# The experts' weights in pieces of 2048 columns, three in flight, with the small operations queued behind stated splits

## The chip, the cores and the metric

The kernel runs on one core of a Trainium2 chip. The metric is the device time in microseconds of one execution of the whole program; lower is better.

## What is computed

A two-layer encoder trunk on 256 tokens of width 1024: in each layer a token mixer with three attention branches, a cross-attention into 256 memory tokens, and a SwiGLU feed-forward part, each followed by a residual and a layer norm. The feed-forward part of the first layer is dense; in the second, every token goes to two of eight experts of hidden width 2816. Only that last part is touched by the change:

```python
def swiglu(t, w_gu, w_down):
    a, g = jnp.split(t @ w_gu, 2, axis=-1)
    return (jax.nn.silu(a) * g) @ w_down
...
    out = jnp.zeros_like(t)
    for e in range(N_EXPERTS):
        out = out + gate[:, e:e + 1] * swiglu(t, w_gu[e], w_down[e])
```

All of it is float32. The kernel reaches that precision with three matmuls in the chip's reduced 32-bit format for each product: every operand is split into a high half (`hi`, a rounded copy) and a low half (`lo`, what the copy lost), and hi x hi, hi x lo and lo x hi are summed.

## The kernel before

The weights lie in memory packed in units, one contiguous load each. `unit` (L184) loads one unit into a `raw` tile (L193), cuts it into pieces, and makes for each piece a hi tile by a ScalarE copy (L203) and a lo tile by a VectorE subtraction (L207). The hi tiles rotate through six places of 1024 columns per partition, the lo tiles through six more, both in the pool `wp`; a place is written again when TensorE has read what was in it. The piece is 1024 columns whatever the unit's shape: two rows of blocks of 512 columns, or four rows of 256. Until the end of the first expert's first step each subtraction is cut in two (`self.cuts`), afterwards it is one instruction.

`experts` (L789) walks over eight experts in six steps j. In a step `up` (L845) makes the gate part `pg` and the linear part `pa` of 512 hidden columns (256 in the sixth step) from the gathered tokens `xg`: each is a chunk of two units of four rows of blocks, so a step has four units. A unit of 512 columns is 2048 columns per partition and gives 12 matmuls of 512 columns; in the sixth step it is 1024 and gives 12 matmuls of 256. `down` (L878) takes the hidden columns of the step before, already turned round in `hT`, through two units (output halves `py`): 2048 columns and 12 matmuls each, in the sixth step two rows of blocks, 1024 columns and 6 matmuls. The order is therefore: up of step 0, up of step 1, down of step 0, up of step 2, down of step 1, and so on across the experts; the sixth `down` of one expert follows the first `up` of the next. Before the first, third, fifth and seventh expert `gather` (L811) fetches the tokens of two experts by matmuls and evacuates them on ScalarE (L835) and VectorE (L836).

What turns `pg` and `pa` into `hT` is put off: `up` appends the function `rest` to the list `self.later`, and `flush` (L872) runs the whole list. `rest` is silu on ScalarE (L862), the product on VectorE (L863), four transposes on TensorE (L866) and a split on ScalarE and VectorE (L243, L244). `flush` is called in `up` once, after the first chunk's splits, and in `down` after the splits of each unit. So the work of step j runs between the splits and the matmuls of the first `down` unit that follows it. After an expert's last `down`, `scatter` (L904) is put off in the same way; it splits the two output halves, scaled by the gate (L246, L247), and after every second expert puts off `add`, 16 matmuls (L921) and four additions (L924) that bring the results back to token order.

Each engine runs its instructions in the order in which they are queued. That order comes from the order of the program text and from a scheduler that may let an instruction whose inputs are late be passed by later ones. All loads are issued on the SP queue.

The three matmuls of a product are:

```python
        t.matmul(out, a[0], b[0], start=first, stop=False, **kw)
        t.matmul(out, a[0], b[1], start=False, stop=False, **kw)
        t.matmul(out, a[1], b[0], start=False, stop=last, **kw)
```

With weights as the moving operand (`a` the tokens, `b` the weights), the first needs the hi tile alone, the second the lo tile, the third the hi tile again.

Of the kernel before, what the change touches and what calls it, by code (L numbers as in the profile page):

```python
# [153 lines left out]
class K:  # L154
    def __init__(self, ctx, tc, I, out):
        self.tc, self.nc, self.I, self.out = tc, tc.nc, I, out
        nc = self.nc
        P = lambda **kw: ctx.enter_context(tc.tile_pool(**kw))
        self.const = P(name="const", bufs=1)
        self.wp = P(name="wp", bufs=3)  # L160
        self.tp = P(name="tp", bufs=1)
        self.nT = 0
        self.xp = P(name="xp", bufs=2)
        self.sm = P(name="sm", bufs=4)
        self.mm = P(name="mm", bufs=3, space=PSUM)
        self.ps = P(name="ps", bufs=2, space=PSUM)
        c = self.const
        self.idn = c.tile([128, 128], FT, name="idn")
        nc.sync.dma_start(self.idn, I["eye"])
        self.half = c.tile([128, 1], FT, name="half")  # L170
        nc.vector.memset(self.half, -0.5)

        self.raws = [(self.wp, "raw")]

        self.cuts = 2
        self.base = {}
        o = 0
        for l in range(DEPTH):
            for p in MIX:
                self.base[p.name, l] = o  # L180
                o += p.size


    def unit(self, src, base, pk, c, g, blocks=False):  # L184


        nc = self.nc
        cn, (k0, kn) = pk.chunks[c][1], pk.groups[g]
        n = kn * cn
        pool, tag = self.raws[0]  # L190
        self.raws.append(self.raws.pop(0))
        raw = pool.tile([128, kn, cn], FT, name="raw", tag=tag, bufs=3 if pool is self.wp else 1)
        nc.sync.dma_start(raw.rearrange("p k c -> p (k c)"),  # L193
                          bass.AP(tensor=src.tensor, offset=src.offset + base + pk.off[c, g], ap=[[n, 128], [1, n]]))
        kp = kn if blocks else 1024 // cn
        out = []
        for a, b in [(0, c) for c in range(cn // 128)] if blocks else [(k, 0) for k in range(0, kn, kp)]:
            ks = slice(a, min(kn, a + kp))
            cs = slice(b * 128, b * 128 + 128) if blocks else slice(0, cn)
            shape = [128, ks.stop - a, cs.stop - cs.start]  # L200
            hi = self.wp.tile(shape, FR, name="hi", tag="hi", bufs=6)
            lo = self.wp.tile(shape, FR, name="lo", tag="lo", bufs=6)
            nc.scalar.activation(hi, raw[:, ks, cs], AF.Copy)  # L203
            m = -(-shape[1] // self.cuts)
            for k in range(0, shape[1], m):
                kk = slice(k, min(k + m, shape[1]))
                nc.vector.tensor_tensor(lo[:, kk], raw[:, a:][:, kk, cs], f32(hi[:, kk]), op=OP.subtract)  # L207
            out.append((k0 + a, shape[1], hi, lo))
        return out

# [7 lines left out]
    def mm3(self, out, a, b, first, last, **kw):  # L218

        t = self.nc.tensor  # L220
        t.matmul(out, a[0], b[0], start=first, stop=False, **kw)  # L221
        t.matmul(out, a[0], b[1], start=False, stop=False, **kw)  # L222
        t.matmul(out, a[1], b[0], start=False, stop=last, **kw)  # L223

    def tm(self, ps, xT, units, t0, KT=8, first=True):

# [562 lines left out]
    def experts(self, c, pos, gs, xs, acc, A, early=()):  # L789

        down, self.later = None, []
        ahead = self.gather(c, 0, pos, xs, A)
        for e in range(E):
            if e % 2 == 0:
                pair = ahead
            one = dict(pair, e=e, i=e % 2, xe=[pair["xg"][e % 2][:, z] for z in range(2)])
            for j in range(6):
                if e == 1 and j == 0:
                    self.raws = [z for z in self.raws if z not in early]
                hT = self.up(one, j, A)  # L800
                self.cuts = 1
                if down:
                    self.down(*down, gs, acc, A)
                down = (one, j, hT)
                if e % 2 and e < E - 1 and j == 1:
                    ahead = self.gather(c, e + 1, pos, xs, A)
        self.down(*down, gs, acc, A)
        while self.later:
            self.flush()

    def gather(self, c, e, pos, xs, A):  # L811

# [32 lines left out]
    def up(self, x, j, A):  # L845

        nc, I = self.nc, self.I
        base = x["e"] * (P_GU.size + P_DN.size)
        n = P_GU.chunks[2 * j][1]
        nb = n // 128  # L850
        pg = self.mm.tile([128, 512], FT, name="pm", tag="mm")
        u = self.chunk(I["we"], base, P_GU, 2 * j + 1)
        self.flush()
        self.tm(pg[:, :n], x["xe"], u, 0)
        u = self.chunk(I["we"], base, P_GU, 2 * j)
        pa = self.mm.tile([128, 512], FT, name="pm", tag="mm")
        self.tm(pa[:, :n], x["xe"], u, 0)
        hT = [A.tile([128, 4, CAP], FR, name="hT" + s) for s in "hl"]

        def rest():  # L860
            h = A.tile([128, 512], FT, name="h", bufs=1)
            nc.scalar.activation(h[:, :n], pa[:, :n], AF.Silu)  # L862
            nc.vector.tensor_tensor(h[:, :n], h[:, :n], pg[:, :n], op=OP.mult)  # L863
            p = self.ps.tile([128, 4, 128], FT, name="pht", tag="t")
            for b in range(nb):
                nc.tensor.transpose(p[:, b], h[:, b * 128:b * 128 + 128], self.idn)  # L866
            self.split(p[:, :nb], *(z[:, :nb] for z in hT))

        self.later.append(rest)
        return hT  # L870

    def flush(self):  # L872

        later, self.later = self.later, []
        for f in later:
            f()

    def down(self, x, j, hT, gs, acc, A):  # L878

        nc, I = self.nc, self.I  # L880
        e, i = x["e"], x["i"]
        base = e * (P_GU.size + P_DN.size) + P_GU.size
        if j == 0:
            self.py = [self.ps.tile([128, 512], FT, name="py", tag="s") for _ in range(2)]
        for cc in range(2):
            u = self.unit(I["we"], base, P_DN, cc, j)
            self.flush()
            for k0, kn, hi, lo in u:
                for k in range(kn):
                    kk = k0 + k  # L890
                    self.mm3(self.py[cc], [z[:, kk - 4 * j] for z in hT], (hi[:, k], lo[:, k]), kk == 0, kk == 21)
        if j == 0:

            p = self.ps.tile([128, 2], FT, name="pgt", tag="t")
            for t in range(2):
                nc.tensor.matmul(p, x["sl"][:, t, i], gs[:, t, e], start=not t, stop=bool(t))
            g2 = self.sm.tile([128, 2], FT, name="g2")
            nc.vector.tensor_copy(g2, p)
            self.g = self.sm.tile([128, 1], FT, name="g1")
            nc.vector.tensor_tensor(self.g, g2[:, 0:1], g2[:, 1:2], op=OP.add)  # L900
        if j == 5:
            self.later.append(lambda: self.scatter(x["st"], e, acc, A))

    def scatter(self, st, e, acc, A):  # L904

# [20 lines left out]
                        self.stats(acc, t, cc)  # L926

        if i:
            self.later.append(add)

    def finish(self, acc, A, name):
        o = self.tp.tile([128, 2, D], FT, name="o" + name, tag=self.xgs[0])
# [6 lines left out]

    def moe(self, x, xT):  # L940
        nc, tc = self.nc, self.tc
        with tc.tile_pool(name="moec", bufs=1) as C:
            acc = x
            with tc.tile_pool(name="moe0", bufs=2) as A:
                pos, gs, xs = self.route(x, xT, C, A)
                nc.scalar.activation(acc, x, AF.Copy, scale=ALPHA)
                T = [f"T{(self.nT + i) % 2}{s}" for i in range(2) for s in "hl"]
                self.xgs = T[:3]

                early = [(self.tp, T[2])] + [(A, "ys" + s) for s in "hl"]  # L950
                self.raws = [(self.wp, "raw")] * 3 + [(A, f"raw{i}") for i in range(5)] + [(self.tp, T[3])] + early
                self.experts(0, pos, gs, xs, acc, A, early)
                self.raws = [(self.wp, "raw")]
                self.finish(acc, A, "a")
            over = nc.values_load(self.over[0:1, 0:1], min_val=0, max_val=S)
            with tc.If(over > CAP):
                with tc.tile_pool(name="moe1", bufs=2) as A:
                    self.experts(1, pos, gs, xs, acc, A)
                    self.finish(acc, A, "b")

    def run(self):
# [7 lines left out]
                self.stats(x, t, i)  # L969
        xT = self.ln_all(x, 0, gb)  # L970
        with ExitStack() as ctx:
            for l in range(DEPTH):
                self.mixer(l, x, xT)
                with tc.tile_pool(name=f"cr{l}", bufs=1) as A:
# [34 lines left out]
```

## Time and profile before

| what | value |
|---|---|
| median of three runs | 1654.68 us (1654.38 to 1655.45) |
| profiled execution, its own time | 1654.94 us |
| its span in the trace | 1652.8 us |
| TensorE matmul, weight load, busy | 97%, 85% |
| VectorE, ScalarE, GpSimd, busy | 80%, 62%, 2% |
| granted TensorE clock, mean | 0.992 |
| read from memory | 418.61 MB, 254 GB/s over the span |

The trace calls TensorE's matmuls PE and its weight loads PEld, VectorE DVE, ScalarE ACT, GpSimd POOL; L207 is line 207 of the kernel. Matmuls are pipelined and their ends are modelled, so their starts say more than their durations. The experts' stage fills the second half of the span, from about 852 us on. Idle time of an engine is put down to the instruction that released it.

### The profile page before, as it was taken

The numbers are of one execution on the slowest core, as the hardware profiler recorded it, in microseconds if no ns is written. First come the engines' busy times: TensorE is split into PE (matmuls) and PEld (weight loads), VectorE is DVE, ScalarE is ACT, GpSimd is POOL, SyncE is SP. The second block draws the span as 40 slices with busy tenths as digits, with TensorE's granted clock in tenths as the row PEclk, the third lists the DMA queues.
The fourth block names the chain that finished last, engine by engine and source line by source line (L and its number), as shares of the span: only waits on it lengthen the run. The fifth ranks groups of instructions, "written<-read, shape, count | busy, mean of one in ns | idle before, by whom it ended". The sixth has DMA issues, their size and how long they took to land.

```text
span 1652.8 us, 24729 instructions
## 1 busy us (share of the span) xinstructions
PE 1607.9 (97%) x9507; PEld 1408.8 (85%) x9507; DVE 1317.8 (80%) x1918; ACT 1022.2 (62%) x1362; POOL 33.4 (2%) x28
## 2 busy tenths in 40 slices
PE   6999999999999999999979999999999999999996
PEld 6999999899998889999868888888888878888785
DVE  7877685765555986777689999998989888989896
ACT  5665444454443575545458777777777677767773
POOL 1100000000000200000000000000000000000000
PEclk9999999999999999999979999999999999999998
DMA  7434564465545533455578888989889898898982
GB/s 272 141 105 152 189 232 167 143 229 180 188 171 198 186 123 131 161 203 205 192 320 328 316 352 321 393 308 382 330 322 372 327 400 325 336 373 314 400 328 84
DMA packets 65647, 421.36 MB, mean 255 GB/s; under 512 B 7664, under 2 KB 8560, under 8 KB 19568
## 3 DMA queue, kind: packets, MB, share of 16 engines
q1 hardware_dynamic: 65520, 419.69, 68.1%
q8 instruction: 77, 1.26, 0.3%
q14 instruction: 50, 0.41, 0.1%
HBM read 418.61 MB, written 1.05 MB: 254 GB/s over the span
## 4 chain that ended last, share of the span: by engine, by line
PE 92%; DVE 5%; issue 1%; ACT 1%; DMA 1%; POOL 0%; SPq 0%; DVEq 0%; ACTq 0%
PE pm L222 20%; PE pm L221 20%; PE pm L223 20%; PE py L223 5%; PE py L222 5%; PE py L221 5%; PE psc L341 2%; DVE lo L207 2%; PE ptr L370 1%; PE pht L866 1%; PE pd L221 1%; PE pd L223 1%; PE pd L222 1%; PE pg L830 1%; PE pp L221 1%; PE pp L222 1%
## 5 line engine op out<-in xcount | busy, mean ns | idle before, releaser
L207 DVE TENSOR_TENSOR lo<-raw,hi 128x1024 fp32r<-128x1024 f32 (+2 forms) x1020 | 935.3, 956 | 187.9 <-ACT hi L203 173.1
L203 ACT ACTIVATE hi<-raw 128x1024 fp32r<-128x1024 f32 x770 | 785.5, 1057 | 311.1 <-PE pm L222 92.1
L222 PE MATMUL pm<-lo,xg 128*128 128x512 f32 (+1 forms) x768 | 286.5, 373 | 2.2 <-DVE lo L207 1.8
L221 PE MATMUL pm<-hi,xg 128*128 128x512 f32 (+1 forms) x768 | 286.4, 373 | 0.0
L223 PE MATMUL pm<-hi,xg 128*128 128x512 f32 (+1 forms) x768 | 285.7, 372 | 0.0
L223 PE MATMUL pm<-xTh,lo 128*128 128x256 f32 x928 | 264.5, 285 | 0.0
L221 PE MATMUL pm<-xTh,hi 128*128 128x256 f32 x928 | 264.4, 285 | 0.0
L222 PE MATMUL pm<-xTl,hi 128*128 128x256 f32 x928 | 264.3, 285 | 0.0
L222 PEld LDWEIGHTS pm<-xTl,hi 128*128 128x128 f32 x928 | 177.8, 192 | 1.1
L221 PEld LDWEIGHTS pm<-xTh,hi 128*128 128x128 f32 x928 | 177.7, 191 | 1.0
L223 PEld LDWEIGHTS pm<-xTh,lo 128*128 128x128 f32 x928 | 177.9, 192 | 0.7
L222 PEld LDWEIGHTS pm<-lo,xg 128*128 128x128 f32 x768 | 144.7, 188 | 30.4 <-DVE lo L207 5.5
L221 PEld LDWEIGHTS pm<-hi,xg 128*128 128x128 f32 x768 | 144.7, 188 | 26.6 <-ACT hi L203 1.3
L223 PEld LDWEIGHTS pm<-hi,xg 128*128 128x128 f32 x768 | 144.7, 188 | 24.8
L221 PE MATMUL py<-hi,hTh 128*128 128x512 f32 x352 | 140.7, 400 | 0.0
L223 PE MATMUL py<-hi,hTl 128*128 128x512 f32 x352 | 140.6, 399 | 0.0
L222 PE MATMUL py<-lo,hTh 128*128 128x512 f32 x352 | 139.6, 397 | 0.0
L862 ACT ACTIVATE h<-pm 128x512 f32<-128x512 f32 (+1 forms) x48 | 27.0, 562 | 121.7 <-PE pm L223 121.7
L222 PEld LDWEIGHTS py<-lo,hTh 128*128 128x128 f32 x352 | 66.1, 188 | 14.7 <-DVE lo L207 0.4
L223 PEld LDWEIGHTS py<-hi,hTl 128*128 128x128 f32 x352 | 66.0, 188 | 14.6
L221 PEld LDWEIGHTS py<-hi,hTh 128*128 128x128 f32 x352 | 66.2, 188 | 13.6
L863 DVE TENSOR_TENSOR h<-h,pm 128x512 f32<-128x512 f32 (+1 forms) x48 | 30.7, 640 | 44.8 <-ACT h L862 44.8
(292 smaller groups left out, 2273.2 us busy)
## 6 DMA issues: line engine op xcount, KB each, us to landing
raw<-in_we SPq DMA_DIRECT2D x240, 1024.0 KB, 6.9
raw<-in_wm SPq DMA_DIRECT2D x84, 1024.0 KB, 4.8
raw<-in_wf SPq DMA_DIRECT2D x32, 1024.0 KB, 4.9
raw<-in_we SPq DMA_DIRECT2D x48, 512.0 KB, 4.9
gb<-in_lnv SPq DMA_DIRECT2D x14, 512.0 KB, 4.7
raw<-in_wm SPq DMA_DIRECT2D x4, 832.0 KB, 5.3
memr<-in_memT SPq DMA_DIRECT2D x3, 1024.0 KB, 4.8
bias<-in_bias SPq DMA_DIRECT2D x8, 256.0 KB, 4.2
```

The costliest lines, as they stand in the source:

```text
L203: nc.scalar.activation(hi, raw[:, ks, cs], AF.Copy)
L207: nc.vector.tensor_tensor(lo[:, kk], raw[:, a:][:, kk, cs], f32(hi[:, kk]), op=OP.subtract)
L221: t.matmul(out, a[0], b[0], start=first, stop=False, **kw)
L222: t.matmul(out, a[0], b[1], start=False, stop=False, **kw)
L223: t.matmul(out, a[1], b[0], start=False, stop=last, **kw)
L341: self.nc.tensor.matmul(p[:, t], q[i][a][:, t * 128:(t + 1) * 128], k[i][b], start=i + a + b == 0, stop=i == n - 1 and a == 1)
L370: nc.tensor.transpose(pt[:, kt, t * 128:(t + 1) * 128], e[:, t, kt * 128:(kt + 1) * 128], self.idn)
L830: nc.tensor.matmul(p[i][:, k % 2], xs[i][:, t, k * 128:k * 128 + 128], sl[:, t].rearrange("p a b -> p (a b)"), start=not t, stop=bool(t))
L862: nc.scalar.activation(h[:, :n], pa[:, :n], AF.Silu)
L863: nc.vector.tensor_tensor(h[:, :n], h[:, :n], pg[:, :n], op=OP.mult)
L866: nc.tensor.transpose(p[:, b], h[:, b * 128:b * 128 + 128], self.idn)
```

## The change

`unit` takes the piece's size from `self.piece`: 1024 columns with six places as before in all other layers, 2048 columns with three places in the experts' stage, where `moe` opens a new pool `hl1` for the hi and lo tiles. Each unit of the experts is then one piece, one ScalarE copy and one VectorE subtraction (two in the first step of the first expert), whether it has 2048 columns or 1024. In the other layers the hi and lo tiles lie in a pool `hl` of their own instead of in `wp`.

`up` calls `flush` after the splits of each of its four units. What is put off now has a count, the number of flushes until it runs: silu and product run in the third (that of the next `up`'s first unit, after the two of `down`), the transposes in the fourth, the split of h in the fifth, `scatter` and `add` in the second. `unit` and `mm3` note the last instruction of each engine in `self.behind`, and `flush` queues what is due behind these instructions on their engines (`issue_after`). `drain` runs what is left: in the first expert's second step, before the last `down`, and at the end.

```diff
+        self.piece = (1024, 6)
+        self.behind = {}
...
-        kp = kn if blocks else 1024 // cn
+        kp = kn if blocks else self.piece[0] // cn
...
-            hi = self.wp.tile(shape, FR, name="hi", tag="hi", bufs=6)
-            lo = self.wp.tile(shape, FR, name="lo", tag="lo", bufs=6)
-            nc.scalar.activation(hi, raw[:, ks, cs], AF.Copy)
+            hi, lo = (self.hl.tile(shape, FR, name=z, tag=z, bufs=self.piece[1]) for z in ("hi", "lo"))
+            self.behind["ACT"] = nc.scalar.activation(hi, raw[:, ks, cs], AF.Copy).ins
...
-                nc.vector.tensor_tensor(lo[:, kk], raw[:, a:][:, kk, cs], f32(hi[:, kk]), op=OP.subtract)
+                self.behind["DVE"] = nc.vector.tensor_tensor(lo[:, kk], raw[:, a:][:, kk, cs], f32(hi[:, kk]),
+                                                             op=OP.subtract).ins
...
-        t.matmul(out, a[1], b[0], start=False, stop=last, **kw)
+        self.behind["PE"] = t.matmul(out, a[1], b[0], start=False, stop=last, **kw).ins
...
                 self.cuts = 1
+                if e == 0 and j == 1:
+                    self.drain()
...
+        self.drain()
         self.down(*down, gs, acc, A)
-        while self.later:
-            self.flush()
+        self.drain()
...
-        pg = self.mm.tile([128, 512], FT, name="pm", tag="mm")
-        u = self.chunk(I["we"], base, P_GU, 2 * j + 1)
-        self.flush()
-        self.tm(pg[:, :n], x["xe"], u, 0)
-        u = self.chunk(I["we"], base, P_GU, 2 * j)
-        pa = self.mm.tile([128, 512], FT, name="pm", tag="mm")
-        self.tm(pa[:, :n], x["xe"], u, 0)
+        pg, pa = (self.mm.tile([128, 512], FT, name="pm", tag="mm") for _ in range(2))
+        for p, ch in ((pg, 2 * j + 1), (pa, 2 * j)):
+            for g in range(2):
+                u = self.unit(I["we"], base, P_GU, ch, g)
+                self.flush()
+                self.tm(p[:, :n], x["xe"], u, 0)
...
+        self.put_off(3, half)
+        self.put_off(4, turn)
+        self.put_off(5, lambda: self.split(hold[0][:, :nb], *(z[:, :nb] for z in hT)))
         return hT
 
     def flush(self):
 
-        later, self.later = self.later, []
-        for f in later:
-            f()
+        due = [f for n, f in self.later if n <= 1]
+        self.later = [(n - 1, f) for n, f in self.later if n > 1]
+        with ExitStack() as ctx:
+            for i in self.behind.values() if due else ():
+                ctx.enter_context(self.tc.issue_after(i))
+            for f in due:
+                f()
+        self.behind = {}
+
+    def put_off(self, n, f):
+        self.later.append((n, f))
+
+    def drain(self):
+        self.behind = {}
+        while self.later:
+            self.flush()
...
-            self.later.append(lambda: self.scatter(x["st"], e, acc, A))
+            self.put_off(2, lambda: self.scatter(x["st"], e, acc, A))
...
-            self.later.append(add)
+            self.put_off(2, add)
...
-        with tc.tile_pool(name="moec", bufs=1) as C:
+        with tc.tile_pool(name="moec", bufs=1) as C, tc.tile_pool(name="hl1", bufs=1) as self.hl:
+            self.piece = (2048, 3)
...
+            self.hl = ctx.enter_context(tc.tile_pool(name="hl", bufs=1))
```

`half` is silu and product, `turn` the four transposes, as they stood in `rest`. The order of the loads does not change.

## Rows read from the trace of the kernel before

**Rows 1.** The page, section 1: busy time of each engine.

```profile
PE 1607.9 (97%) x9507; PEld 1408.8 (85%) x9507; DVE 1317.8 (80%) x1918; ACT 1022.2 (62%) x1362; POOL 33.4 (2%) x28
```

**Rows 2.** Busy time by stretches of the expert stage.

```profile
core 0: us, PE busy (x) PEld busy (x) DVE busy (x) ACT busy (x) POOL busy (x), PEclk, DMA share, GB/s
...
1000.00:1100.00 100.00, 99.99 (x471) 82.20 (x471) 92.18 (x88) 78.05 (x82) 0.00 (x0) 1.00 0.92 355
...
1400.00:1500.00 100.00, 100.00 (x472) 82.60 (x471) 86.85 (x87) 70.64 (x80) 0.00 (x0) 1.00 0.90 349
```

**Rows 3.** Waits, expert stage: who, for whom, total, times, longest.

```profile
ACT h L862 <- PE pm L223: 121.7, 47, 4.4
...
PEld pm L222 <- DVE lo L207: 5.5, 9, 1.1
...
PE pm L222 <- DVE lo L207: 1.8, 3, 0.8
```

**Rows 4.** Timeline, TensorE: start us, us, instruction.

```profile
1001.19 0.39 PE L221 MATMUL pm<-hi,xg 128*128 128x512 f32 x1
...
1006.40 0.40 PE L223 MATMUL pm<-hi,xg 128*128 128x512 f32 x1
...
1008.50 0.61 PE L866 MATMUL pht<-idn,h 128*128 128x128 f32 x4
...
1009.18 0.39 PE L221 MATMUL py<-hi,hTh 128*128 128x512 f32 x1
...
1011.98 0.39 PE L221 MATMUL py<-hi,hTh 128*128 128x512 f32 x1
...
1029.66 0.28 PE L221 MATMUL pm<-hi,xg 128*128 128x256 f32 x1
...
1035.17 0.28 PE L222 MATMUL pm<-lo,xg 128*128 128x256 f32 x1
```

**Rows 5.** Timeline, TensorE after the scatter.

```profile
1350.38 0.50 PE L221 MATMUL pm<-hi,xg 128*128 128x512 f32 x1
1351.64 0.50 PE L222 MATMUL pm<-lo,xg 128*128 128x512 f32 x1 [0.76 <-DVE lo L207]
...
1354.64 0.40 PE L221 MATMUL pm<-hi,xg 128*128 128x512 f32 x1
1355.17 0.50 PE L222 MATMUL pm<-lo,xg 128*128 128x512 f32 x1
```

**Rows 6.** The page, section 6: DMA issues of the experts' weights.

```profile
raw<-in_we SPq DMA_DIRECT2D x240, 1024.0 KB, 6.9
```

**Rows 7.** Timeline, ScalarE; idle time and its releaser in brackets.

```profile
1001.39 1.06 ACT L203 ACTIVATE hi<-raw 128x1024 fp32r<-128x1024 f32 x1 [0.29 <-PE pm L223]
...
1009.23 0.58 ACT L243 ACTIVATE hTh<-pht 128x512 fp32r<-128x512 f32 x1
...
1349.28 1.05 ACT L203 ACTIVATE hi<-raw 128x1024 fp32r<-128x1024 f32 x1
```

**Rows 8.** Groups by form, whole span: the split of 2048 columns.

```profile
L244 DVE TENSOR_TENSOR meml<-memr,memh 128x2048 fp32r<-128x2048 f32 x3 | 6.9, 2287 | 0.6 <-ACT memh L243 0.6
...
L243 ACT ACTIVATE memh<-memr 128x2048 fp32r<-128x2048 f32 x3 | 5.8, 1920 | 2.3 <-DVE mTl L247 2.3
```

**Rows 9.** Timeline, VectorE.

```profile
1350.36 1.23 DVE L207 TENSOR_TENSOR lo<-raw,hi 128x1024 fp32r<-128x1024 f32 x1 [0.20 <-ACT hi L203]
...
1353.90 9.16 DVE L207 TENSOR_TENSOR lo<-raw,hi 128x1024 fp32r<-128x1024 f32 x8
```

**Rows 10.** Groups by form, whole span: VectorE's other operations of 512 columns.

```profile
L207 DVE TENSOR_TENSOR lo<-raw,hi 128x512 fp32r<-128x512 f32 x484 | 315.8, 685 | 157.6 <-ACT hi L203 154.6
...
L863 DVE TENSOR_TENSOR h<-h,pm 128x512 f32<-128x512 f32 x40 | 27.4, 684 | 39.6 <-ACT h L862 39.6
...
L247 DVE SCALAR_TENSOR_TENSOR ysl<-py,g,ysh 128x512 fp32r<-128x512 f32 x16 | 11.9, 746 | 5.7 <-ACT ysh L246 5.7
```

**Rows 11.** Timeline, TensorE in a gather.

```profile
1175.05 0.50 PE L830 MATMUL pg<-sl,xsh 128*128 128x256 f32 x2 [0.41 <-ACT xg L835]
```

More of the change, by code (lines that the diff above doesn't have):

```diff
@@ L850, in up, with half, turn @@
         nb = n // 128
-        pg = self.mm.tile([128, 512], FT, name="pm", tag="mm")
-        u = self.chunk(I["we"], base, P_GU, 2 * j + 1)
-        self.flush()
-        self.tm(pg[:, :n], x["xe"], u, 0)
-        u = self.chunk(I["we"], base, P_GU, 2 * j)
-        pa = self.mm.tile([128, 512], FT, name="pm", tag="mm")
-        self.tm(pa[:, :n], x["xe"], u, 0)
+        pg, pa = (self.mm.tile([128, 512], FT, name="pm", tag="mm") for _ in range(2))
[4 more added lines that the diff above has]
+                self.tm(p[:, :n], x["xe"], u, 0)
         hT = [A.tile([128, 4, CAP], FR, name="hT" + s) for s in "hl"]
-        def rest():
-            h = A.tile([128, 512], FT, name="h", bufs=1)
+        h = A.tile([128, 512], FT, name="h", bufs=1)
+        hold = [None]
+        def half():
             nc.scalar.activation(h[:, :n], pa[:, :n], AF.Silu)
             nc.vector.tensor_tensor(h[:, :n], h[:, :n], pg[:, :n], op=OP.mult)
-            p = self.ps.tile([128, 4, 128], FT, name="pht", tag="t")
+        def turn():
+            hold[0] = self.ps.tile([128, 4, 128], FT, name="pht", tag="t")
             for b in range(nb):
-                nc.tensor.transpose(p[:, b], h[:, b * 128:b * 128 + 128], self.idn)
-            self.split(p[:, :nb], *(z[:, :nb] for z in hT))
-        self.later.append(rest)
+                nc.tensor.transpose(hold[0][:, b], h[:, b * 128:b * 128 + 128], self.idn)
+        self.put_off(3, half)
+        self.put_off(4, turn)
+        self.put_off(5, lambda: self.split(hold[0][:, :nb], *(z[:, :nb] for z in hT)))
         return hT
     def flush(self):
-        later, self.later = self.later, []
-        for f in later:
-            f()
+        due = [f for n, f in self.later if n <= 1]
[12 more added lines that the diff above has]
+            self.flush()
     def down(self, x, j, hT, gs, acc, A):
```

## The prediction

> **What bounds the kernel now.** I read the page's busy line first [rows 1]: TensorE is called busy 97% of the span. That alone proves little, since ends of matmuls are modelled, so I went on by stage. In the expert stage, from about 852 to 1640 us, TensorE is never idle, VectorE is busy 0.92 of the time early and 0.87 late, POOL does nothing and the granted clock is 1.00, the level of 2.4 GHz [rows 2]. The waits tell who is late: ScalarE stands 121.7 us in front of the silu for TensorE to finish its sum, while TensorE waited for VectorE three times, 1.8 us together, and its weight loads nine times, 5.5 us [rows 3]. The third view is the start-to-start step of matmuls: 23 steps from 1001.19 to 1006.40 give 0.2265 us for an `up` matmul of 512 columns, 12 steps from 1009.18 to 1011.98 give 0.2333 us for a `down` matmul, and 46 steps from 1029.66 to 1035.17 give 0.120 us for 256 columns [rows 4]. They are even: TensorE sets the pace, and the splits run ahead of it until they meet an occupied piece. The exceptions are few. After the scatter at 1350 a lo half is late, 1.26 where 0.23 is the step, then 0.53 for 0.23 [rows 5]: 1.03 + 0.30 = 1.33 us, and the same pattern stands once more at 1548; the third wait of the three [rows 3] adds some 0.3. So only about 3 us of this stage are there to win from earlier splits.
>
> [...]
>
> **The piece and the ring.** A unit is one load: 2048 columns per partition for 240 units [rows 6], 1024 for the other 48, six per expert (the sixth `up` step has 256 columns, the sixth `down` step two rows of blocks). Before, each full unit was two pieces in a ring of six; now every unit is one piece, long or short, in a ring of three. A short unit was one place of six and is now one place of three: that decides my forecast. A piece is refilled when TensorE has read it. The links, from rows:
> - ScalarE starts 0.20 after the next piece's first matmul: 1001.19 to 1001.39 [rows 4, 7].
> - The hi half takes 1.06 for 1024 columns [rows 7] and 1.92 for 2048, by the one split of that size [rows 8].
> - VectorE starts 0.03 after it: 1349.28 + 1.05 to 1350.36 [rows 7, 9].
> - The lo half takes 1.23 for 1024 [rows 9], 2.29 for 2048 [rows 8].
> - TensorE goes on 0.05 later: 1350.36 + 1.23 to 1351.64 [rows 5, 9].
>
> Refill before: 0.20 + 1.06 + 0.03 + 1.23 + 0.05 = 2.57 us, under five pieces of 1.36 us or more, 6.8. Refill after: 0.20 + 1.92 + 0.03 + 2.29 + 0.05 = 4.49 us, under two pieces. The lo half is wanted at the second matmul, so one step of 0.23 is added to the cover:
> - two full `up` pieces, 2 x 12 x 0.2265 + 0.23 = 5.67: spare 1.18, no wait;
> - two short `up` pieces, 2 x 12 x 0.12 + 0.23 = 3.11: late by **1.38**;
> - two short `down` pieces, 2 x 6 x 0.2333 + 0.23 = 3.03: late by **1.46**.
>
> A full piece follows two short ones twice per expert: the fifth `down` behind the sixth `up` (8 times), and the next expert's second `up` behind the sixth `down` (7 times, the last expert has none after it). 8 x 1.38 + 7 x 1.46 = **+21.3 us**. A refill cannot start sooner, whatever the order of the queues, and TensorE has no other work of that length at these places.
>
> **The moved small operations.** Before, silu, product, transposes and the split of h came together in the next flush. Now silu and product come behind the third unit's splits, the transposes behind the fourth's matmuls, the split of h behind the fifth's; no DMA moves with them, and the loads keep their order on SP. Count from the first matmul of a step's `down`. The silu stands behind a hi half that waits for the very piece that ended the sum, so it no longer blocks; the 121.7 us of ScalarE go, but they were no one's path: 0. The worst added wait is hTh: behind it in ScalarE's queue stands the fourth `up` unit's hi half. The transposes start at 2 x 2.80 + 2.72 = 8.32, hTh 0.73 later and frees the engine after 0.50 [rows 4, 7], so the unit is ready at 9.55 + 1.92 + 0.03 + 2.29 + 0.05 = 13.84. TensorE wants it at 8.32 + 0.45 + 2 x 2.72 + 0.23 = 14.44 (four transposes cost 0.45: 1008.50 to 1009.18 less one step [rows 4]). Spare 0.60: nothing.
>
> The scatter has less room. Its two splits stand on VectorE behind the second unit of the step that has just lost 1.46. Engine time is a duration less the 0.10 that overlaps (1.23 against (9.16 - 1.23) / 7 = 1.13 in a row of eight [rows 9]): lo 2.19, product 0.58, scaled split 0.65 [rows 8, 10]. The first lo starts at 2.15 (0.20 + 1.92 + 0.03), and 2.15 + 3 x 2.19 + 0.58 + 2 x 0.65 + 0.10 + 0.05 = 10.75 for the third unit. TensorE wants it at 4.49 + 11 x 0.2265 + 0.45 + 2.72 + 0.23 = 10.38. Late 0.37, 7 times: **+2.6**. The late lo halves of today at the scatter go: **-3.0** (2 x 1.33 + 0.3).
>
> The three gathers in the stage stop today for 0.41 at an evacuation by ScalarE [rows 11]. A hi half in front of it is 0.86 longer, a lo half on VectorE's side 1.06. Between 0 and 1.9 each; I take 1.0, nearer to the ScalarE row that ends the wait now: **+3.0**.
>
> Costed at nothing: the two early drains (0 to 3 us once: the last `down` may find its splits behind hTh; they are ready sooner and should stand in front). The start of the stage: the first expert's lo halves grow from 0.69 to 1.23 [rows 9, 10] and stand between operations of the router; late by up to 0.54 for each of 7, +3.8, or 0.5 better by fewer instructions; I take 0 since the sum of columns is the same. The places of the pools in SBUF move: `up` and `down` matmuls of the same shape differ by 0.007 us per step [rows 4]. If that is their place, 1056 `down` matmuls could gain 7.2 and 1920 `up` matmuls could lose 13.1; I take 0, today's values. Other layers keep 1024 in six.
>
> **Sum.** 21.3 + 2.6 - 3.0 + 3.0 = +23.9. The profiled execution took 1654.94 (span 1652.8), 0.26 over the median: 1654.94 + 23.9 = 1678.8, against the median **1678.6 us**. By the bounds: down to 1668 (gathers 0, `down` steps better, 0.5 at the start), up to 1698 (`up` steps worse, start and gathers at their ends).
>
> **The rivals.**
> - **VectorE is the bound, and it ends faster.** Place: the stage's lo halves; price: two of 1024 cost 2 x 1.13 of engine time, one of 2048 2.19, so 0.07 to 0.08 for 236 units, 17 us: **1638**. It decides if TensorE's steps today hide a wait for VectorE. For: 0.92 busy [rows 2]. Against: 1.8 us of waits [rows 3], even steps [rows 4].
> - **Three pieces cover it.** The ring refills sooner than I think at short units (two could share a place, or the late ones get filled with transposes). Then only today's 3 us go: **1651**.
> - **The split of h blocks.** If the transposes come after the fourth unit's matmuls instead of before them, hTh waits 2.72 longer and eats the spare 0.60: late 2.1 in some 40 steps, 85 us more: **1764**. Against: they come first in the text and h is ready 3 us before.
> - **Not in effect**: the orders come out as the text of before has them, and only the pieces grow. Then silu, 0.50 like hTh, stands in front of the second `down` unit's hi half, which is ready at 0.20 + 0.50 + 4.29 = 4.99 where TensorE wants it at 2.80 + 0.23 = 3.03: late 1.96 in 46 steps, 90 us, **1769**. Against: today nothing is late behind the silu for so long [rows 3].
>
> The Trainium skill (Perfetto Trace Analysis, Optimizing Scalar/DVE Operations) gives about 60 ns of overhead per VectorE instruction and advises larger operations when that engine is saturated; an estimate from that figure is 236 x 0.06 = 14 us, which by that rule alone gives 1641. The same section says that where these engines are not saturated but make bubbles on others, smaller instructions finish sooner. That speaks against this change. The trace agrees with the figure (0.07 to 0.08 per unit) and with the second rule's case: rows 3 show VectorE late for 1.8 us only.
>
> **How the numbers follow.** Forecast 0.70, VectorE the bound 0.08, cover suffices 0.13, split of h blocks 0.05, not in effect 0.04. A measurement here tells 0.2%, 3.3 us, from no change. Faster: 0.08 + two thirds of 0.13 + 0.01 of the forecast's tail = 0.18; same 0.05; slower 0.77. Forecast's own range: 1668 to 1698. To leave out no more than 2 in 10 it must reach the second rival: **1649 to 1698**.
>
> **What would show it.** Right: lo and hi of 128x2048 at 2.29 and 1.92; gaps of some 1.4 us at the second matmul of the fifth `down` and of the next expert's second `up`, each released by VectorE's lo; no gap between full pieces; the ACT wait in front of silu gone; steps of 0.2265 and 0.2333 elsewhere. Wrong: no gaps behind short pieces (rival two), gaps in every step (rival three), steps shorter than 0.2265 (rival one), or other steps all through (SBUF places).

## The result and the profile after

The changed kernel takes **1680.8 us** (median of four runs, 1679.08 to 1681.94), the kernel before 1654.53 us on the same chip: 1.0157 times, interval 1.014 to 1.0175, or 26.3 us more. The forecast was 1678.6, with a range of 1649 to 1698. The profiled execution took 1680.59 us, its span is 1678.7.

The busy line of the page, after (lines have moved: L206 is the hi half, L210 the lo half, L225 to L227 the three matmuls, L868 silu, L874 the transposes, L247 the split of h on ScalarE):

```profile
PE 1611.8 (96%) x9507; PEld 1406.5 (84%) x9507; DVE 1300.8 (77%) x1674; ACT 999.7 (60%) x1122; POOL 32.9 (2%) x28
```

Beside [rows 1], VectorE does 1674 instructions for 1918 and is busy 17.0 us less, and ScalarE 22.5 us less. Nobody gets that time. The stretches of the expert stage, with the columns of [rows 2]:

```profile
1000.00:1100.00 100.00, 97.85 (x456) 79.80 (x455) 84.42 (x56) 68.78 (x51) 0.00 (x0) 1.00 0.90 343
...
1400.00:1500.00 100.00, 97.13 (x455) 79.41 (x454) 84.30 (x55) 68.63 (x50) 0.00 (x0) 1.00 0.91 342
```

VectorE is down from 92.18 to 84.42, and TensorE, 99.99 before, is now short of 2 to 3 us in a hundred at the same granted clock. From the first expert's first matmul to the last matmul of the last scatter the stage takes 851.12 to 1663.15, 812.03 us; before it was 851.36 to 1637.51, 786.15. That is 25.9 us more, as much as the spans differ (1678.7 - 1652.8). That the stage begins at the same time in both kernels is chance, as shown below.

Waits, 860 to 1660 us (who, for whom: total, times, longest):

```profile
ACT hi L206 <- PE pm L227: 144.8, 149, 4.6
...
PE pm L226 <- DVE lo L210: 10.3, 7, 1.6
...
PE py L226 <- DVE lo L210: 5.5, 5, 1.3
...
PE py L225 <- ACT hi L206: 2.9, 4, 0.7
...
PE pg L836 <- ACT xg L841: 1.7, 4, 0.7
...
ACT h L868 <- PE pm L227: 0.8, 1, 0.8
```

The wait in front of silu has gone from 121.7 us to 0.8, and ScalarE's time now stands in front of the hi half, where it waits for a free piece. TensorE, which waited three times for a lo half [rows 3], now waits for a half of a piece at sixteen places: seven at an `up` (10.3), eight at a fifth `down` (four by its lo half, four by its hi half), and once at the early drain, which makes the fifth of the `py` waits for a lo half.

**The gap at the second `up`,** early in the stage, TensorE's timeline:

```profile
1061.86 0.40 PE L227 MATMUL py<-hi,hTl 128*128 128x512 f32 x1
1062.10 0.39 PE L225 MATMUL pm<-hi,xg 128*128 128x512 f32 x1
1063.86 0.50 PE L226 MATMUL pm<-lo,xg 128*128 128x512 f32 x1 [1.38 <-DVE lo L210]
```

The first matmul of the unit needs the hi half alone and starts in step; the second stands 1.76 behind it where a step is 0.23: 1.53 lost. The bracket says 1.38, because it counts from the modelled end of the matmul before. Starts are the better measure. The same place late in the stage, on TensorE, ScalarE and VectorE:

```profile
1569.26 0.40 PE L226 MATMUL py<-lo,hTh 128*128 128x512 f32 x1
...
1571.77 0.39 PE L225 MATMUL pm<-hi,xg 128*128 128x512 f32 x1
1573.75 0.50 PE L226 MATMUL pm<-lo,xg 128*128 128x512 f32 x1 [1.59 <-DVE lo L210]
```

```profile
1569.45 1.92 ACT L206 ACTIVATE hi<-raw 128x2048 fp32r<-128x2048 f32 x1 [1.98 <-PE pm L227]
```

```profile
1571.41 2.29 DVE L210 TENSOR_TENSOR lo<-raw,hi 128x2048 fp32r<-128x2048 f32 x1 [2.67 <-ACT hi L206]
```

This is the refill chain link by link. ScalarE had been idle for 1.98 and VectorE for 2.67, so neither was behind with its work; they had no piece to write to. The piece comes free when TensorE starts on the next one, at 1569.26; the hi half starts at 1569.45, the lo half 0.04 after its end, TensorE 0.05 after that: 4.49 from 1569.26 to 1573.75, as the prediction added it up. The loss here is 1.98 - 0.23 = 1.75, since the scheduler had let TensorE do one `py` matmul earlier, ahead of the short units' time, and the cover is one step shorter.

**The gap at the fifth `down`,** TensorE:

```profile
1041.15 0.40 PE L225 MATMUL py<-hi,hTh 128*128 128x512 f32 x1
1042.28 0.49 PE L225 MATMUL py<-hi,hTh 128*128 128x512 f32 x1 [0.73 <-ACT hi L206]
1042.81 0.50 PE L226 MATMUL py<-lo,hTh 128*128 128x512 f32 x1
```

Four of the eight experts look like this: while the lo half is missing, TensorE takes the first matmul of the other output half, waits for that one's hi half, and then goes on. From 1041.15 to 1042.81 two steps pass: 1.66 - 2 x 0.23 = 1.20 lost. In the other four it takes nothing, and loses 1.43.

**The steps have changed too,** and not only at the gaps. An `up` and a `down` step, TensorE:

```profile
1012.50 0.39 PE L225 MATMUL py<-hi,hTh 128*128 128x512 f32 x1
...
1017.72 0.40 PE L227 MATMUL py<-hi,hTl 128*128 128x512 f32 x1
...
1021.41 0.39 PE L226 MATMUL pm<-lo,xg 128*128 128x512 f32 x1
...
1029.35 0.40 PE L227 MATMUL pm<-hi,xg 128*128 128x512 f32 x1
```

23 `down` steps take 5.22, 0.227 each, and 34 `up` steps 7.94, 0.2335 each. Before it was the other way round [rows 4]: `up` 0.2265, `down` 0.2333.

**The start of the stage** comes at nearly the same time, 851.12 for 851.36, but two changes hide each other in it. The last matmul ahead of the router (the part that assigns the tokens to experts) and the first expert's first matmul, on TensorE, before and after:

```profile
827.18 0.40 PE L223 MATMUL pm<-hi,oTl 128*128 128x512 f32 x1
...
851.36 0.39 PE L221 MATMUL pm<-hi,xg 128*128 128x512 f32 x1
```

```profile
823.56 0.40 PE L227 MATMUL pm<-hi,oTl 128*128 128x512 f32 x1
...
851.12 0.50 PE L225 MATMUL pm<-hi,xg 128*128 128x512 f32 x1
```

The layers ahead of the stage are 3.6 us faster. Their pieces are as before, but their hi and lo tiles lie elsewhere and the steps of their matmuls have changed (last section); an estimate from those steps gives 3.1. The way from there into the stage takes 27.56 for 24.18, 3.4 more. VectorE, after:

```profile
836.16 0.14 DVE L749 TENSOR_TENSOR lg<-lg,pr 128x8 f32<-128x8 f32 x1
836.24 1.21 DVE L210 TENSOR_TENSOR lo<-raw,hi 128x1024 fp32r<-128x1024 f32 x1
837.37 0.15 DVE L752 MAX8 mx<-lg 128x8 f32<-128x8 f32 x1
```

The first expert's lo halves stand between the router's small operations, and each takes 1.2 us where it took 0.7 [rows 10]. Of all kernels of this document, the six with pieces of 2048 take 27.2 to 28.5 us for this way, the seven with pieces of 1024 take 23.4 to 24.9.

### The profile page after: what moved, and what is told of

Its sections match the earlier page's. It is cut to its first block, busy times and chain, and to the rows that moved or that the text cites. A ratio compares the mean times of both kernels' runs of the same rounds, so it can differ in the third digit from the quotient of the medians.

```text
span 1678.7 us, 24069 instructions
## 1 busy us (share of the span) xinstructions
PE 1611.8 (96%) x9507; PEld 1406.5 (84%) x9507; DVE 1300.8 (77%) x1674; ACT 999.7 (60%) x1122; POOL 32.9 (2%) x28
## 4 chain that ended last, share of the span: by engine, by line
PE 88%; DVE 6%; ACT 3%; DMA 1%; issue 1%; POOL 0%; SPq 0%; DVEq 0%; ACTq 0%
PE pm L226 20%; PE pm L227 20%; PE pm L225 20%; PE py L226 4%; PE py L227 4%; PE py L225 4%; DVE lo L210 3%; ACT hi L206 2%; PE psc L345 2%; PE ptr L374 1%; PE pht L874 1%; PE pd L227 1%; PE pd L225 1%; PE pd L226 1%; PE pp L225 1%
## 5 line engine op out<-in xcount | busy, mean ns | idle before, releaser
L210 DVE TENSOR_TENSOR lo<-raw,hi 128x512 fp32r<-128x512 f32 (+2 forms) x776 | 920.3, 1211 | 275.7 <-ACT hi L206 271.5
L206 ACT ACTIVATE hi<-raw 128x1024 fp32r<-128x1024 f32 (+2 forms) x530 | 762.7, 1445 | 475.4 <-PE pm L227 193.4
L226 PE MATMUL pm<-lo,xg 128*128 128x512 f32 (+1 forms) x768 | 290.0, 378 | 10.3 <-DVE lo L210 10.3
L225 PE MATMUL pm<-hi,xg 128*128 128x512 f32 (+1 forms) x768 | 293.2, 382 | 0.1
L227 PE MATMUL pm<-hi,xg 128*128 128x512 f32 (+1 forms) x768 | 289.0, 376 | 0.0
L227 PE MATMUL pm<-xTh,lo 128*128 128x256 f32 x928 | 263.5, 284 | 0.0
L225 PE MATMUL pm<-xTh,hi 128*128 128x256 f32 x928 | 263.2, 284 | 0.0
L225 PEld LDWEIGHTS pm<-xTh,hi 128*128 128x128 f32 x928 | 174.9, 188 | 1.0
L227 PEld LDWEIGHTS pm<-xTh,lo 128*128 128x128 f32 x928 | 175.0, 189 | 0.7
L227 PEld LDWEIGHTS pm<-hi,xg 128*128 128x128 f32 x768 | 144.3, 188 | 28.4
L225 PEld LDWEIGHTS pm<-hi,xg 128*128 128x128 f32 x768 | 144.4, 188 | 27.3 <-ACT xg L841 0.3
L225 PE MATMUL py<-hi,hTh 128*128 128x512 f32 x352 | 137.9, 392 | 2.9 <-ACT hi L206 2.9
L227 PE MATMUL py<-hi,hTl 128*128 128x512 f32 x352 | 137.5, 391 | 0.1
L225 PEld LDWEIGHTS py<-hi,hTh 128*128 128x128 f32 x352 | 66.1, 188 | 18.3 <-ACT hi L206 4.2
L227 PEld LDWEIGHTS py<-hi,hTl 128*128 128x128 f32 x352 | 66.1, 188 | 14.0 <-DVE hTl L248 0.4
L225 PE MATMUL pm<-hi,xTh 128*128 128x256 f32 (+2 forms) x128 | 42.8, 336 | 2.3 <-DVE x L285 1.6
L227 PE MATMUL pm<-hi,xTl 128*128 128x256 f32 (+2 forms) x128 | 42.3, 331 | 0.3 <-DVE xTl L248 0.3
```

The source lines that it names most:

```text
L206: self.behind["ACT"] = nc.scalar.activation(hi, raw[:, ks, cs], AF.Copy).ins
L210: self.behind["DVE"] = nc.vector.tensor_tensor(lo[:, kk], raw[:, a:][:, kk, cs], f32(hi[:, kk]), op=OP.subtract).ins
L227: self.behind["PE"] = t.matmul(out, a[1], b[0], start=False, stop=last, **kw).ins
```

## The experiments

Ratios are to runs of the kernel before on the same chip, with their 95% interval. The theory: a ring of three places gives two pieces of cover, a short piece is a whole place, and so a refill of 4.49 us comes late behind two short units. The rivals for the 26 us: the queueing with its waits; the size of the instructions itself; the places of the tiles in SBUF, which the steps above point to.

**Six places of 1024 instead of three of 2048**, all else as in the changed kernel.

```diff
-            self.piece = (2048, 3)
+            self.piece = (1024, 6)
```

> The changed kernel with the pieces of the experts' stage back at 1024 columns in six places; the new queueing and the new pools stay. If the ring of three is the cause (a short unit takes one place of three), every gap behind two short units goes, 12.5 us at the fifth down and 12.1 us at the second up, with 1.0 us more at the third unit: 1680.8 - 25.6 = about 1655 us, with the matmul steps of the changed kernel (0.233 us up, 0.227 us down). If the queueing of the small operations were the cause, the gaps would stay and the time with them: 1675 us or more.

Measured: 1653.63 (1652.78 to 1654.8), 0.9992 (0.9983 to 1.0002). The fifth `down` of the same expert, TensorE's timeline:

```profile
1033.69 0.28 PE L227 MATMUL pm<-hi,xg 128*128 128x256 f32 x1
1033.81 0.40 PE L225 MATMUL py<-hi,hTh 128*128 128x512 f32 x1
1034.05 0.40 PE L226 MATMUL py<-lo,hTh 128*128 128x512 f32 x1
```

No gap, here or at any other unit. The bytes of SBUF are the same and the queueing is the new one; five pieces of cover are back for two. Against the changed kernel 27 us are gone: 24.3 in the stage (787.75 for 812.03) and 2.6 ahead of it (its first matmul is at 848.53 for 851.12). The pieces and the ring carry the 26 us. The `up` step stays at 0.233.

**The queueing of before, with pieces of 2048 in three.** `up`, `flush` and the lists are those of the kernel before.

```diff
...
-        self.put_off(3, half)
-        self.put_off(4, turn)
-        self.put_off(5, lambda: self.split(hold[0][:, :nb], *(z[:, :nb] for z in hT)))
+        self.later.append(rest)
...
```

> The changed kernel's pieces and pools, with silu, product, transposes and the split of h put off and flushed as in the kernel before. If the ring is the cause, the gaps behind short units stay, and the silu that waits for its sum comes on top of them: slower than the changed kernel, between 1681 us and the 1769 us of the rival worked out in the prediction. If the new queueing were the cause of the gaps, it would be near 1656 us.

Measured: 1682.58 (1681.32 to 1683.71), 1.0167 (1.015 to 1.0184). The gaps are there without the new queueing; the second `up`, TensorE (L925 is a matmul of the scatter, which fills a part):

```profile
1061.67 0.40 PE L225 MATMUL pm<-hi,xg 128*128 128x512 f32 x1
...
1063.36 0.50 PE L226 MATMUL pm<-lo,xg 128*128 128x512 f32 x1 [0.82 <-DVE lo L210]
```

The run also tests what silu does in its old place under the large pieces, the premise of the prediction's fourth rival. ScalarE:

```profile
1008.82 1.92 ACT L206 ACTIVATE hi<-raw 128x2048 fp32r<-128x2048 f32 x1 [0.88 <-PE pm L227]
1011.62 0.60 ACT L866 ACTIVATE h<-pm 128x512 f32<-128x512 f32 x1 [0.88 <-PE pm L227]
1012.12 1.91 ACT L206 ACTIVATE hi<-raw 128x2048 fp32r<-128x2048 f32 x1
```

The second `down` unit's hi half (1008.82) has gone ahead of the silu; behind it stands only a hi half that waits for the same end of the sum. It loses 0.50 of a spare of 1.18. So the 1.96 per step of that rival, 90 us in all, was never there to be had: an order worked out from the text alone had put the silu one unit too early.

**Two short `up` units as one piece.** The two loads of 1024 columns of a sixth-step chunk land in one tile and are split at once; `flush` is called twice behind it, so that what is put off runs where it did. The short `down` units stay. (`unit`, which does the two loads, is left out here.)

```diff
-            for g in range(2):
-                u = self.unit(I["we"], base, P_GU, ch, g)
+            for g in range(2) if nb == 4 else (0,):
+                u = self.unit(I["we"], base, P_GU, ch, g, both=nb < 4)
...
```

> The changed kernel with the two short units of each chunk of the sixth up step loaded side by side into one piece of 2048 columns (two loads, one copy, one subtraction), so that no short piece stands before the fifth down; the short units of the sixth down step stay. Ring: the gaps at the fifth down go (12.5 us), those at the second up stay at 1.5 to 1.75 us: about 1668 us. If the size of the instruction or the queueing made the gaps, both kinds stay: 1681 us.

Measured: 1666.87 (1666.06 to 1668.54), 1.0072 (1.0055 to 1.0088), some 14 us less than the changed kernel. The stage takes 800.63 for 812.03, 11.4 less, which is what the gaps at the fifth `down` and the steps behind them come to (10.5 + 0.9). Of the rest, 2.1 lie behind the last matmul of the last scatter (13.46 us to the end for 15.51, and 15.3 to 15.5 in the other runs); why is not shown. The gaps at the fifth `down`, which stands behind the merged units, are gone. Those at the second `up`, behind the short `down` units that were left, are the same as ever; TensorE:

```profile
1058.97 0.39 PE L228 MATMUL pm<-hi,xg 128*128 128x512 f32 x1
1060.74 0.50 PE L229 MATMUL pm<-lo,xg 128*128 128x512 f32 x1 [1.38 <-DVE lo L213]
```

One cause taken away, one of the two kinds of gaps goes: it is the short pieces, each where it stands, and not the large instruction as such.

**Four places of 2048.** To make room, the experts' loads go through two landing tiles (`raw`) fewer; those alone, with three places, are the control.

```diff
-            self.piece = (2048, 3)
+            self.piece = (2048, 4)
...
-                self.raws = [(self.wp, "raw")] * 3 + [(A, f"raw{i}") for i in range(5)] + [(self.tp, T[3])] + early
+                self.raws = [(self.wp, "raw")] * 3 + [(A, f"raw{i}") for i in range(3)] + [(self.tp, T[3])] + early
```

> The changed kernel with four places of 2048 columns instead of three; the room comes from two of the tiles that loads land in (nine instead of eleven from the second expert on). Ring: a refill of 4.49 us then lies under three pieces, at the worst two short ones and a full one, 2.81 + 2.72 us, so the gaps of 12.5 and 12.1 us go although the pieces stay long: about 1656 us. If the length of the pieces made the gaps (refill itself too slow), they stay: 1680 us.

> The control of the run with four places: the changed kernel with its three places and the same two landing tiles fewer. Loads land in 6.6 us and nine tiles are 20 us of work or more, so nothing should change: 1681 us. If the loads were close to late, it would be slower, and the run with four places would have to be read against this one.

Measured: four places 1660.86 (1659.74 to 1661.52), 1.0037 (1.0023 to 1.005); the control 1679.99, 1.0154 (1.0138 to 1.0169), so the landing tiles do nothing. The gaps at the second `up` are gone. At the fifth `down` 0.50 is left in six experts, which I had not expected; TensorE, then ScalarE:

```profile
1236.65 0.40 PE L225 MATMUL py<-hi,hTh 128*128 128x512 f32 x1
1237.38 0.50 PE L226 MATMUL py<-lo,hTh 128*128 128x512 f32 x1 [0.33 <-DVE lo L210]
```

```profile
1232.60 0.60 ACT L247 ACTIVATE hTh<-pht 128x512 fp32r<-128x512 f32 x1 [0.68 <-PE pht L874]
1233.10 5.51 ACT L206 ACTIVATE hi<-raw 128x2048 fp32r<-128x2048 f32 x3
```

With a place free earlier, the hi half could start earlier, but the split of h is queued ahead of it and waits for the transposes: ScalarE idles 0.68 and then works 0.50. That is the added wait that the prediction had examined for full units. With three places the missing place hides it; with four it is next in line. These six gaps and the steps behind them come to 3.6 us; another 3.6 of the distance to the run with six of 1024 lie ahead of the stage, whose first matmul is at 852.17 here and at 848.53 there.

**32 bytes in front of the tiles.** An unused tile of 32 bytes per partition in the pool `moec` shifts what is allocated after it, in the changed kernel and in the kernel before; 64 bytes in the kernel before are the control.

```diff
             acc = x
+            C.tile([128, 8], FT, name="place")
             with tc.tile_pool(name="moe0", bufs=2) as A:
```

> The changed kernel with 32 unused bytes per partition ahead of the pools of the experts' stage: hi, lo and hT tiles then begin at the same offset modulo 256 bytes as the tokens xg. If that offset sets the step of a matmul, up matmuls fall from 0.233 to 0.227 us (1920 of them, 12 us) and down matmuls stay at 0.227: about 1668.5 us, with the gaps untouched. If not the offset but the distance or the order of the pools matters, nothing changes: 1681 us.

> The kernel before with the 32 unused bytes ahead of the pool of the experts' stage, nothing else. hT then begins at the same offset modulo 256 bytes as the hi and lo tiles, as the tokens did already. If that offset sets the step, down matmuls fall from 0.2333 to 0.227 us (1056 of them, 6.7 us) and up matmuls stay: about 1648 us. If not, 1654.7 us.

> The control of the place: the kernel before with 64 unused bytes instead of 32, so that hT begins at another offset modulo 256 bytes than hi and lo again. If equal offsets are what counts, 1654.5 us with down steps of 0.233 us; if any move of the pool helps, 1650.5 us as with 32 bytes.

Measured: the changed kernel with 32 bytes 1670.76 (1669.74 to 1671.75), 1.0095 (1.0078 to 1.0112), 10.0 us less than without; the kernel before with 32 bytes 1650.53 (1648.86 to 1651.86), 0.9974 (0.9963 to 0.9985), 3.8 less than its own runs; with 64 bytes 1654.44, 0.9998 (0.9989 to 1.0007), nothing. The gaps of the changed kernel are as they were; its `up` steps are not. TensorE:

```profile
1020.05 0.39 PE L227 MATMUL pm<-hi,xg 128*128 128x512 f32 x1
...
1026.17 0.39 PE L227 MATMUL pm<-hi,xg 128*128 128x512 f32 x1
```

27 steps in 6.12, 0.2267 each, for 0.2335.

**The queueing alone, with and without the 32 bytes.** Pieces of 1024 in six, in the pools of the kernel before.

```diff
-        with tc.tile_pool(name="moec", bufs=1) as C, tc.tile_pool(name="hl1", bufs=1) as self.hl:
-            self.piece = (2048, 3)
+        with tc.tile_pool(name="moec", bufs=1) as C:
...
-            self.hl = ctx.enter_context(tc.tile_pool(name="hl", bufs=1))
+            self.hl = self.wp
```

> The new queueing alone, on the pools and the pieces of before (1024 columns, six places), without the 32 bytes. The late lo halves behind the scatter go (3 us), up steps stay at 0.227 and down steps at 0.233 us as in the kernel before: about 1651 us. If the queueing is worth nothing by itself, 1654.5 us; if it costs at other places (the gathers), more than that.

> The new queueing with the pieces of before (1024 columns, six places, in the pool of before) and the 32 bytes of place. No gaps behind short units (as with six of 1024), none of the 3 us behind the scatter, up and down steps at 0.227 us: the run with six of 1024 (1653.6 us) less 1920 x 0.0065 = 12.5 us, about 1641 us, faster than both kernels. If places did not matter here, 1653 us.

Measured: the queueing alone 1652.32 (1651.21 to 1653.65), 0.9985 (0.9976 to 0.9994), a gain of 2.4 us; with 32 bytes 1645.9 (1644.37 to 1646.15), 0.9945 (0.9931 to 0.9959). The 1641 that I had put down for the latter asked too much. It took 12.5 for the `up` steps, where their mean over the stage, 0.2332 with six of 1024 and 0.2274 here, gives 11.1; and in the pools of before the stage begins at 851.09, not at 848.53. By the ratios the bytes give 0.0040 x 1654.5 = 6.6 here and 3.8 to 4.3 with the old queueing. The intervals alone do not tell these apart; the steps of the last section do.

**Everything that helped:** the changed kernel with six places of 1024 and 32 bytes.

> Six pieces of 1024 columns in the changed kernel's pools, with the 32 bytes: the two levers found so far on the changed kernel. The run with six of 1024 took 1653.6 us with up steps of 0.233 us; with 0.227 us for 1920 of them 12 us go: about 1642 us. If the 32 bytes do nothing here, 1653.6 us.

Measured: **1643.35** (1642.53 to 1644.14), 0.9927 (0.9913 to 0.994), faster than both kernels. Groups by form, 860 to 1660 us, of this kernel:

```profile
L226 PE MATMUL pm<-lo,xg 128*128 128x512 f32 x625 | 243.6, 390 | 0.0
...
L226 PE MATMUL py<-lo,hTh 128*128 128x512 f32 x352 | 137.2, 390 | 0.0
```

The same two groups of the changed kernel:

```profile
L226 PE MATMUL pm<-lo,xg 128*128 128x512 f32 x628 | 249.4, 397 | 10.3 <-DVE lo L210 10.3
...
L226 PE MATMUL py<-lo,hTh 128*128 128x512 f32 x352 | 138.2, 393 | 5.6 <-DVE lo L210 5.5
```

The idle time in front is gone, and both mean durations are at the lower value.

## Why the prediction was right, and where it was not

**The main step held.** Its gaps came at the two places named, 8 and 7 times, and nowhere between full pieces. By starts they are 4 x 1.20 + 4 x 1.43 = 10.5 at the fifth `down` (predicted 8 x 1.38 = 11.0) and 4 x 1.53 + 3 x 1.75 = 11.4 at the second `up` (7 x 1.46 = 10.2), together 21.9 for 21.3. The size follows from the chain and the steps as they now are: 4.49 - (2 x 12 x 0.118 + 0.23) = 1.43, and 4.49 - (2 x 6 x 0.227 + 0.23) = 1.54. That "TensorE has no other work of that length at these places" was nearly so: it found one matmul in four of the fifteen. Not counted were some 0.10 more at the step behind each gap, 1.6 in all.

The other terms, worked out from all start-to-start steps of TensorE, before and after:

| term | predicted, us | measured, us |
|---|---|---|
| gaps behind two short units, and the step behind each | +21.3 | +23.5 |
| scatter: third unit late, and the step behind | +2.6 | +0.9 |
| late lo halves of before at the scatter, and the steps behind | -3.0 | -4.6 |
| three gathers | +3.0 | +0.6 |
| early drains | 0 (0 to 3) | +1.1 |
| layers ahead of the stage (to their last matmul, 827.18, now 823.56) | 0 | -3.6 |
| start of the stage (24.18, now 27.56) | 0 (-0.5 to +3.8) | +3.4 |
| 1920 `up` steps of 512, 0.2273 to 0.2332 | 0 (to +13.1) | +11.3 |
| 1056 `down` steps, 0.2330 to 0.2279 | 0 (to -7.2) | -5.4 |
| 384 `up` steps of 256, 0.1198 to 0.1181 | 0 | -0.7 |
| transposes and the steps next to them | 0 | -0.9 |
| sum | +23.9 | +25.6 |

The spans differ by 25.9, of which 0.2 lies behind the last scatter. The four terms that the prediction added up to 23.9 measure 20.4 together, and those that it put at nothing give 5.2. That the number came out so near is luck; that the gaps came, where and how long, is not.

- **SBUF places, "I take 0, today's values", failed,** and it is the largest miss. Both ends of the bound happened at once and left about +5. The layers ahead of the stage, which the prediction passed over with "Other layers keep 1024 in six", moved as well and gave 3.6 back. The experiment with 32 bytes agrees: it brings the changed kernel's `up` steps back and gives 10.0.
- **The start of the stage, "I take 0 since the sum of columns is the same", was mis-sized** and hidden by the line above it: +3.4, near the end of the bound, by the very mechanism that the prediction had named for that end.
- **Scatter, +2.6, was mis-sized.** The unit is late by about 0.17 after three of the seven scatters, for 0.37 after all; 0.10 at the step behind it, after four, makes 0.9. The order on VectorE was the predicted one. I did not follow where the missing 0.2 went.
- **The late lo halves of before, -3.0, were under-read.** Between the two that the prediction counted [rows 5] stands a third, and the step behind each is longer too; TensorE, before:

```profile
1352.91 0.39 PE L221 MATMUL pm<-hi,xg 128*128 128x512 f32 x1
1353.37 0.50 PE L222 MATMUL pm<-lo,xg 128*128 128x512 f32 x1
1353.71 0.39 PE L223 MATMUL pm<-hi,xg 128*128 128x512 f32 x1
```

Such a place costs 1.9 by starts, not 1.33; there are two, and 0.7 at three others.

- **Gathers, +3.0, were too dear.** Each was allowed up to 1.9; two take 0.7 and 0.5 longer than before, the third 0.6 less.
- **Early drains at 0:** one wait, 0.57 at the late matmul and 0.48 at the two behind it. The bound of 0 to 3 held.
- **The moved transposes, counted without a gain, gave 0.9.** In the kernel before a pair of them started 0.40 behind the matmul ahead of it (1036.57 to 1036.97); now it is 0.23 (1560.17 to 1560.40).

**The rivals.** *VectorE is the bound:* its busy time fell by just the 17 us that the rival priced, and no time came of it; the even steps of [rows 4] had told the truth, and 0.92 busy had not. The Trainium skill (Perfetto Trace Analysis, Optimizing Scalar/DVE Operations) distinguishes a saturated VectorE, for which larger operations can improve throughput, from one that is not saturated but makes bubbles on other engines, for which broken-up instructions may let work finish sooner. The runs stand on the second side: 1653.63 with 1024 in six, 1680.8 with 2048 in three. *Three pieces cover it:* excluded by the gaps, and by what the four places and the merged units change. *Split of h blocks:* the transposes do come ahead of the fourth unit's matmuls (1020.74, 8.24 after the step's first `down` matmul; 8.32 was put down), and no step of full units is late for it; with four places it is what is left at the fifth `down`, 0.50. *Not in effect:* the wait at silu is gone, and the price was wrong besides, as the old queueing under large pieces shows.

## What to carry to other kernels

Count a ring's cover in time, not in places: refill chain (free to ready, through every engine) against the shortest run of pieces that can stand in the ring. Making pieces larger at equal bytes lengthened the chain here from 2.57 to 4.49 us and left two pieces of cover for five, too few wherever short pieces stand in the ring; so an engine that is busy 0.92 of the time but late for nobody is best left with its small instructions. And compare start-to-start steps of the same matmul before and after any change of pools: 3% of a step, over 3000 matmuls, was worth more than the queueing.

## What the runs showed of the hardware

The step of a 512-column matmul takes one of two values, and it goes with where the two operands' tiles begin in a partition. Below are the mean steps in the stage (the dozen matmuls behind a transpose left out) beside the first byte's offset, modulo 256, of the stationary and the moving tile as the program lays them out:

| kernel | `up` offsets | step, us | `down` offsets | step, us |
|---|---|---|---|---|
| before; queueing alone | 160, 160 | 0.2271; 0.2272 | 128, 160 | 0.2332; 0.2333 |
| before + 64 bytes | 160, 160 | 0.2272 | 192, 160 | 0.2329 |
| before + 32 bytes | 160, 160 | 0.2271 | 160, 160 | 0.2272 |
| changed; six of 1024 | 160, 128 | 0.2331; 0.2331 | 128, 128 | 0.2274; 0.2273 |
| changed + 32 bytes | 160, 160 | 0.2272 | 160, 160 | 0.2271 |
| six of 1024 + 32 bytes | 160, 160 | 0.2269 | 160, 160 | 0.2272 |

Equal offsets go with the short step in every layout that ran, unequal ones with the long step. The layers ahead of the stage agree, and the change itself moved their tiles: the dense layer's `down` goes from 0.2324 at 32, 160 to 0.2267 at 32, 32, and the matmuls on `mT` from 0.2270 at 160, 160 to 0.2323 at 160, 32. Since 32 and 160 are equal modulo 128, equality modulo 128 is not enough. Matmuls of 256 columns go the other way: 0.1195 to 0.1199 at equal offsets, 0.1181 to 0.1190 at unequal ones. Why is not shown, and only these offsets ran. A second effect stands beside it: where the step is short, matmuls in the dozen behind a group of transposes take 0.229 to 0.230 (in the kernel before with 32 bytes, `down` 0.2300 behind them, 0.2272 elsewhere). With the 32 bytes the mean of all `down` steps falls from 0.2331 to 0.2286 under the old queueing, which has the transposes in `down`, and from 0.2333 to 0.2271 under the new one, which has them in `up`: 4.8 and 6.5 us for 1056 steps. That is most of the difference between 3.8 and 6.6. The cause of this effect is open too.
